# The opening's root mean squares: sums in all partitions, roots on full rows, no spread

## The chip, the cores and the metric

The kernel runs on one core of a Trainium2 chip. The metric is the device time of one execution in microseconds (us); of several runs the median is given. The engines are TensorE (PE in the profile, its weight loads PEld), VectorE (DVE), ScalarE (ACT), GpSimd (POOL) and SyncE (SP, whose queue issues the transfers). Each engine runs its own list of instructions in order; an instruction that waits holds up all that stand behind it on its engine.

## The reference

One encoder layer is applied to two groups of tokens, 2048 and 512, each with 16 learned meta tokens ahead. All of it is in f32.

```python
def rms_norm(x, g):
    x32 = x.astype(jnp.float32)
    y = x32 * lax.rsqrt(jnp.mean(x32 * x32, axis=-1, keepdims=True) + RMS_EPS)
    return (y * g.astype(jnp.float32)).astype(x.dtype)

def mixer_layer(h, norm_g, w_in, ...):
    u = rms_norm(h, norm_g)
    proj = u @ w_in
    qa, ka, va, za, qb, kb, vb, zb, ga, gb = jnp.split(proj, cuts, axis=-1)
    ... # neighbourhood attention on qa, ka, va; windowed attention on qb, kb, vb; gates; projections
```

The change is in how the first `rms_norm` gets its factor, the reciprocal root of each token's mean square over 1024 features.

## The kernel before

Features lie in partitions and tokens in columns, five windows of 512 tokens. A matrix is split into a high part in a short f32 format (fp32r) and the rest, and a product is three TensorE products: high by high, high by low, low by high (`mm3`, lines 146 to 148). The last window (number 4, with the meta tokens as 16 further columns) is projected alone; the first four go in pairs by Strassen's scheme.

The **opening** is the function `beside`: it projects window 4 for 22 tiles f of 128 output features (0 to 3 are qa, 4 to 7 qb, then ka, va, kb, vb), while VectorE and ScalarE make the Strassen operands of windows 0 and 1. One tile is 24 products in four steps of six, and the steps are counted in `q`. Two lists of step numbers in the call say when the generators `prep_last` (window 4's own preparation) and `prep_first` (that of windows 0 and 1) go on. The order on TensorE and in SP's queue is as written; the order on the other three engines is set when the program is built.

What the prediction touches:

- **Banks.** A tile's products add up in one of five PSUM banks (`ps_mm`, name `mm`). Window 4 is projected before it is normalised: the bank is emptied by `combine` (line 288), a VectorE product with `rs`, the row of factors, into `tq` or `tkv`. So no bank comes free before `rs` is there. Stores of the first tiles are held until step 14.
- **Weights.** A tile's weights land in `wraw`; ScalarE casts the high part and VectorE subtracts for the low part, in two halves (lines 207 and 208), into one of two buffers `wt`. Tile f+1's are made while f is projected, in the buffer of f-1.
- **The sums of squares.** ScalarE squares; VectorE adds up `rs` for window 4 (line 349) and `rsp` for window 0 (line 430), GpSimd `rsp` for window 1. The squares `sq` lie in the pool `ev`, four buffers that later also hold `evq`, the split queries on their way to memory.
- **The factors.** For window 4, `prep_last` at step 9 sums `rs` over the partitions by five f32 products with a column of ones, which put 128 tokens into partitions each; ScalarE copies the 128x5 sums; `rsqrt` (lines 153 to 163) takes the roots by three rounds on 128x5; `diagonal` (line 177) lays them on diagonals `rs_dg`; at step 14 five f32 products of ones with these (`spread`, line 185) put every token's factor into all partitions, and ScalarE copies it to `rs`. For windows 0 and 1, `prep_first` does the same at steps 20 and 27 with eight columns.
- **The operands.** From step 28 on VectorE scales windows 0 and 1 with these factors (line 384), adds and subtracts, and splits (388 and 389).

Of the kernel before, what the change touches and what calls it, by code (L numbers as in the profile page):

```python
# [17 lines left out]
P = 128  # L18
# [77 lines left out]
def encoder_block(ctx: ExitStack, tc: tile.TileContext, xT, x_end, w_in, w_pa, w_pb, w_o, norm_g, final_g,  # L96
# [25 lines left out]
    def f32(ap):  # L122
        return ap.bitcast(F32)
# [70 lines left out]

    wpool = ctx.enter_context(tc.tile_pool(name="wpool", bufs=2))
# [21 lines left out]
    class Weights:  # L217
# [12 lines left out]
        def split(self, i):  # L230
            if i < len(self.srcs):
                self.wt[i] = split_w(self.raw.pop(i))
# [91 lines left out]
    def prep_last(meta):  # L324
# [36 lines left out]
        nc.vector.tensor_add(rs[:, WTOK:], b[:, 0], b[:, 1])  # L361
        yield
        sq = st.tile([P, 32], F32, tag="sq", name="sq", bufs=1)[:, :5]
        nc.vector.memset(sq, 1.0)
        v = ps_t.tile([P, WTOK], F32, tag="vt", name="fin_v")
        for c in range(4):
            nc.tensor.matmul(v[:, c : c + 1], rs[:, c * P : (c + 1) * P], ones[:, 0:1], start=True, stop=True)
        nc.tensor.matmul(v[:N_META, 4:5], rs[:, WTOK:], ones[:, 0:1], start=True, stop=True)
        nc.scalar.copy(sq[:, :4], v[:, :4])
        nc.scalar.copy(sq[:N_META, 4:5], v[:N_META, 4:5])  # L370
        r = rsqrt(uxp, sq, P, 5)
        dgs = [ev.tile([P, WTOK], F32, tag="t", name="rs_dg", bufs=3) for _ in range(2)]
        diagonal(dgs[0], r[:, :4], P)
        diagonal(dgs[1], r[:N_META, 4:5], N_META)
        yield
        for dg, c0, m, nc_ in (dgs[0], 0, P, 4), (dgs[1], WTOK, N_META, 1):
            nc.scalar.copy(rs[:, c0 : c0 + nc_ * m], spread(ps_t, "vt", dg, m, nc_)[:, : nc_ * m])
# [26 lines left out]
    def prep_first(sp, wa, loaded):  # L404
# [27 lines left out]
        v = ps_t.tile([P, WTOK], F32, tag="vt", name="fin_v")  # L432
        for i in range(2):
            for c in range(4):
                nc.tensor.matmul(v[:, 4 * i + c : 4 * i + c + 1], rss[i][:, c * P : (c + 1) * P], ones[:, 0:1],
                                 start=True, stop=True)
        r = rsqrt(uxp, v[:, :8], P, 8)
        dgs = [ev.tile([P, WTOK], F32, tag="t", name="rs_dg", bufs=3) for _ in range(2)]
        for i in range(2):
            diagonal(dgs[i], r[:, 4 * i : 4 * i + 4], P)  # L440
        yield
        for i in range(2):
            nc.scalar.copy(rss[i], spread(ps_t, "vt", dgs[i], P, 4))
# [1358 lines left out]
```

## Time and profile before

| | before |
|---|---|
| median of 3 runs (lowest, highest) | 1874.19 us (1873.26, 1876.14) |
| the profiled execution | 1877.09 us, its span 1875.3 us |
| TensorE busy | 1852.4 us (99%) |
| VectorE, ScalarE, GpSimd busy | 1319.5, 1147.8, 778.4 us |
| first product of the opening | 7.22 us |
| first Strassen product | 123.52 us |

A row of the timeline gives the start in us from the span's beginning, the length in us, the engine, the line in the kernel, the operation, output and inputs, shapes and, behind an x, how many instructions were put together; in brackets the idle time ahead and what ended it. TensorE's instructions overlap: the distance of two starts is what one costs. A row of the waits gives who waited for whom, us in total, times, and the longest. Of a row by tile or line the three numbers are the shortest, median and longest duration in ns. A row by stretches gives the busy time of PE, PEld, DVE, ACT and POOL in this order, then the granted clock, the share of the transfer engines and GB/s.

### The profile page before, as it was taken

What the parts mean: (1) busy time and instruction counts of PE and PEld (TensorE: products, weight loads), DVE (VectorE), ACT (ScalarE), POOL (GpSimd) and SP (SyncE); (2) the same over time, 40 slices, a digit from 0 to 9 for tenths busy, and PEclk for the clock granted to TensorE, in tenths of its full rate; (3) what the DMA queues carried; (4) which work ended last, traced back from release to release, by engine and by line L of the source; (5) the groups of instructions that cost most, each with busy time, mean ns of one, the idle gap of its engine ahead of it and who ended that gap; (6) DMA issues with size and microseconds to landing.
All of it is one profiled execution on the core that took longest, in us unless ns stands there. A gap on an engine that the chain in (4) does not pass through costs nothing.

```text
span 1875.3 us, 29643 instructions
## 1 busy us (share of the span) xinstructions
PE 1852.4 (99%) x9755; PEld 1579.9 (84%) x9755; DVE 1319.5 (70%) x2914; ACT 1147.8 (61%) x2531; POOL 778.4 (42%) x599
## 2 busy tenths in 40 slices
PE   8999999999999999999999999999999999999998
PEld 6998888888888888888878888888888888888887
DVE  8886667556476565444457788878887877888874
ACT  6454444444365444444456797798789778878932
POOL 2015443323203232322324435657855874786420
PEclk9999999999999999999999999999999999999999
DMA  7565756655295677644258869968996997698483
GB/s 260 190 182 211 206 172 189 212 180 180 84 338 191 188 224 201 200 138 160 107 187 297 277 206 279 301 215 246 326 290 196 296 301 250 206 310 280 131 298 134
DMA packets 288145, 414.35 MB, mean 221 GB/s; under 512 B 117736, under 2 KB 162360, under 8 KB 286456
## 3 DMA queue, kind: packets, MB, share of 16 engines
q1 hardware_dynamic: 287704, 412.45, 68.6%
q8 instruction: 78, 1.28, 0.3%
q14 instruction: 75, 0.61, 0.1%
q10 hardware_dynamic: 288, 0.01, 0.0%
HBM read 303.46 MB, written 108.91 MB: 220 GB/s over the span
## 4 chain that ended last, share of the span: by engine, by line
PE 89%; DMA 5%; DVE 3%; ACT 1%; issue 1%; SPq 1%; ACTq 0%; DVEq 0%
PE pa L867 24%; PE pe L867 12%; PE pc L867 6%; PE mm L148 3%; PE mm L147 3%; PE mm L146 3%; PE pso L146 3%; PE pso L148 3%; PE pso L147 3%; PE tp L1283 3%; PE tp L1169 2%; PE psa L146 2%; PE psa L148 2%; PE psa L147 2%; PE psb L148 2%; PE psb L146 2%
## 5 line engine op out<-in xcount | busy, mean ns | idle before, releaser
L208 POOL TENSOR_TENSOR wt<-wraw,wt 128x512 fp32r<-128x512 f32 x164 | 212.3, 1314 | 249.1 <-ACT wt L207 233.0
L867 PE MATMUL pa<-u,wt 128*128 128x512 f32 x1008 | 242.8, 389 | 0.3 <-DVE wt L208 0.3
L867 PE MATMUL pa<-u,x 128*128 128x512 f32 x984 | 236.5, 389 | 0.0
L207 ACT CAST wt<-wraw 128x512 fp32r<-128x512 f32 x312 | 178.0, 619 | 76.8 <-DMA wraw<-in_w_in_dram 36.5
L867 PEld LDWEIGHTS pa<-u,wt 128*128 128x128 f32 x1008 | 189.0, 188 | 39.9 <-DVE wt L208 0.8
L867 PEld LDWEIGHTS pa<-u,x 128*128 128x128 f32 x984 | 184.7, 188 | 38.4
L836 POOL TENSOR_TENSOR s<-wraw,raw 128x512 f32<-128x512 f32 x40 | 58.3, 1458 | 277.2 <-DVE x L208 277.2
L146 PE MATMUL mm<-u,wt 128*128 128x512 f32 (+2 forms) x416 | 150.5, 362 | 7.2 <-ACT u L341 7.2
L147 PE MATMUL mm<-u,wt 128*128 128x512 f32 (+2 forms) x416 | 146.8, 353 | 1.0 <-DVE u L342 1.0
L148 PE MATMUL mm<-u,wt 128*128 128x512 f32 (+2 forms) x416 | 146.8, 353 | 0.3 <-DVE wt L208 0.2
L208 DVE TENSOR_TENSOR wt<-wraw,wt 128x512 fp32r<-128x512 f32 x148 | 104.8, 745 | 53.4 <-ACT wt L207 52.9
L867 PE MATMUL pe<-u,wt 128*128 128x512 f32 x504 | 121.3, 390 | 0.0
L867 PE MATMUL pc<-u,wt 128*128 128x512 f32 x504 | 121.1, 389 | 0.0
L867 PE MATMUL pe<-u,x 128*128 128x512 f32 x480 | 115.3, 389 | 0.0
L1172 ACT CAST ph<-tp 128x384 fp32r<-128x384 f32 (+6 forms) x160 | 81.8, 511 | 52.1 <-PE tp L1169 50.7
L841 POOL TENSOR_TENSOR s<-wraw,s 128x512 f32<-128x512 f32 x42 | 56.4, 1342 | 136.9 <-DVE wt L208 136.3
L867 PEld LDWEIGHTS pc<-u,wt 128*128 128x128 f32 x504 | 94.6, 188 | 19.6
L867 PEld LDWEIGHTS pe<-u,wt 128*128 128x128 f32 x504 | 94.5, 188 | 19.6
L146 PE MATMUL pso<-mh,wt 128*128 128x512 f32 x256 | 107.5, 420 | 0.0
L1068 DVE CUSTOM_DVE_ANT_0 s<-s,ba 128x384 f32<-128x384 f32 (+5 forms) x160 | 86.8, 543 | 29.1 <-PE s L1146 26.7
L1173 DVE TENSOR_TENSOR pl<-tp,ph 128x384 fp32r<-128x384 f32 (+6 forms) x160 | 94.9, 593 | 16.4 <-ACT ph L1172 13.6
L867 PEld LDWEIGHTS pe<-u,x 128*128 128x128 f32 x480 | 90.1, 188 | 18.7
(274 smaller groups left out, 5029.0 us busy)
## 6 DMA issues: line engine op xcount, KB each, us to landing
wraw<-in_w_in_dram SPq DMA_DIRECT2D x86, 512.0 KB
raw<-in_w_in_dram SPq DMA_DIRECT2D x40, 512.0 KB
q<-qa SPq DMA_DIRECT2D x40, 512.0 KB
wraw<-in_w_o_dram SPq DMA_DIRECT2D x32, 512.0 KB
kbt<-kb SPq DMA_DIRECT2D x32, 384.0 KB
qa<-evq SPq DMA_DIRECT2D x20, 512.0 KB
qb<-evq SPq DMA_DIRECT2D x20, 512.0 KB
ka<-evk SPq DMA_DIRECT2D x20, 512.0 KB
```

The lines of the kernel that those rows point to most:

```text
L146: nc.tensor.matmul(ps, wh, uh, start=first, stop=False)
L147: nc.tensor.matmul(ps, wh, ul, start=False, stop=False)
L148: nc.tensor.matmul(ps, wl, uh, start=False, stop=last)
L207: high[0] = nc.scalar.copy(h, r).ins
L208: low[0] = (eng or lo_eng[0]).tensor_sub(l, r, f32(h)).ins
L836: eng.tensor_sub(s3, a11, a21)
L841: eng.tensor_sub(s4, a12, s2)
L867: nc.tensor.matmul(ps, wt[:, a, s], u[:, b, kk, :], start=first and kk == 0 and i == 0, stop=kk == 3 and i == 2, skip_group_check=True)
L1068: nc.vector.tensor_tensor_reduce(s[:, :n], s[:, :n], bias, -1.0, 3.0e38, ALU.add, ALU.min, nm)
L1172: nc.scalar.copy(ph_[:kb, a], tb)
L1173: nc.vector.tensor_sub(pl_[:kb, a], tb, f32(ph_[:kb, a]))
L1283: nc.tensor.transpose(tp[:, c + h * P : c + (h + 1) * P], prs[:, k0[h] + j * P : k0[h] + (j + 1) * P], ident)
```

## The change

- Window 4: ScalarE and VectorE split `rs` into `rsh`. At step 10, not 9, two products of 512 columns of ones with the two parts (`by_ones`, lines 191 and 192) give the sums in all 128 partitions at once; the meta tokens' sums are an f32 product of 16 columns. At step 14, ScalarE makes the mean square `y` and -1/2 of it, `hv` (128x528); VectorE takes the roots on 128x528: one guess and three rounds of three operations. There is no diagonal, no spread and no copy.
- Windows 0 and 1: at step 20 the two sums are split into `rsq`; at step 22 four products with ones; then ScalarE makes the mean squares, VectorE the guesses, and two rounds of another iteration follow with five steps on ScalarE and five on GpSimd for each window. The spread at step 27 goes.
- In `dense_fin`, later in the kernel, only names change.

```diff
+    def guess(r, ve):
+        nc.vector.tensor_scalar(r.bitcast(I32), ve.bitcast(I32), -0.5, float(0x5F3759DF), ALU.mult, ALU.add)
...
         nc.vector.tensor_add(rs[:, WTOK:], b[:, 0], b[:, 1])
-        yield
-        sq = st.tile([P, 32], F32, tag="sq", name="sq", bufs=1)[:, :5]
-        nc.vector.memset(sq, 1.0)
-        v = ps_t.tile([P, WTOK], F32, tag="vt", name="fin_v")
-        for c in range(4):
-            nc.tensor.matmul(v[:, c : c + 1], rs[:, c * P : (c + 1) * P], ones[:, 0:1], start=True, stop=True)
-        nc.tensor.matmul(v[:N_META, 4:5], rs[:, WTOK:], ones[:, 0:1], start=True, stop=True)
-        nc.scalar.copy(sq[:, :4], v[:, :4])
-        nc.scalar.copy(sq[:N_META, 4:5], v[:N_META, 4:5])
-        r = rsqrt(uxp, sq, P, 5)
-        dgs = [ev.tile([P, WTOK], F32, tag="t", name="rs_dg", bufs=3) for _ in range(2)]
-        diagonal(dgs[0], r[:, :4], P)
-        diagonal(dgs[1], r[:N_META, 4:5], N_META)
-        yield
-        for dg, c0, m, nc_ in (dgs[0], 0, P, 4), (dgs[1], WTOK, N_META, 1):
-            nc.scalar.copy(rs[:, c0 : c0 + nc_ * m], spread(ps_t, "vt", dg, m, nc_)[:, : nc_ * m])
+        e = ev.tile([P, 2, WTOK], F32R, tag="ev", name="rsh")
+        split(e[:, 0, :], e[:, 1, :], rs[:, :WTOK])
+        yield
+        v = by_ones(ps_t, "vt", e[:, 0, :], e[:, 1, :], "fin_v")
+        vm = ps_t.tile([P, WTOK], F32, tag="vt", name="fin_m")[:, :N_META]
+        nc.tensor.matmul(vm, ones, rs[:, WTOK:], start=True, stop=True)
+        y, hv = (ev.tile([P, 2, WTOK], F32, tag="ev", name=n).rearrange("p i t -> p (i t)")[:, :UW]
+                 for n in ("rsy", "rshv"))
+        for dst, k in (y, 1.0), (hv, -0.5):
+            nc.scalar.activation(dst[:, :WTOK], v, AF.Copy, bias=k * EPS, scale=k / D_MODEL)
+            nc.scalar.activation(dst[:, WTOK:], vm, AF.Copy, bias=k * EPS, scale=k / D_MODEL)
+        guess(rs, y)
+        for _ in range(3):
+            nc.vector.tensor_mul(y, rs, hv)
+            nc.vector.tensor_mul(y, y, rs)
+            nc.vector.scalar_tensor_tensor(rs, y, 1.5, rs, ALU.add, ALU.mult)
+        yield
         yield
...
-        v = ps_t.tile([P, WTOK], F32, tag="vt", name="fin_v")
+        parts = []
         for i in range(2):
-            for c in range(4):
-                nc.tensor.matmul(v[:, 4 * i + c : 4 * i + c + 1], rss[i][:, c * P : (c + 1) * P], ones[:, 0:1],
-                                 start=True, stop=True)
-        r = rsqrt(uxp, v[:, :8], P, 8)
-        dgs = [ev.tile([P, WTOK], F32, tag="t", name="rs_dg", bufs=3) for _ in range(2)]
+            e = ev.tile([P, 2, WTOK], F32R, tag="ev", name="rsq")
+            split(e[:, 0, :], e[:, 1, :], rss[i])
+            parts.append((e[:, 0, :], e[:, 1, :]))
+        yield
         for i in range(2):
-            diagonal(dgs[i], r[:, 4 * i : 4 * i + 4], P)
-        yield
-        for i in range(2):
-            nc.scalar.copy(rss[i], spread(ps_t, "vt", dgs[i], P, 4))
+            v = by_ones(ps_t, "vt", *parts[i], "fin_v")
+            nc.scalar.activation(tts[:, i], v, AF.Copy, bias=EPS, scale=1.0 / D_MODEL)
+            guess(rss[i], tts[:, i])
+        temps = [ev.tile([P, 2, WTOK], F32, tag="ev", name="rt") for _ in range(2)]
+        both = [(rss[i], tts[:, i], temps[i][:, 0], temps[i][:, 1]) for i in range(2)]
+        mul, act = nc.gpsimd.tensor_mul, nc.scalar.activation
+        for step in (lambda r, ve, y, t: act(y, r, AF.Square), lambda r, ve, y, t: mul(y, y, ve),
+                     lambda r, ve, y, t: act(t, y, AF.Copy, scale=0.375, bias=-1.25), lambda r, ve, y, t: mul(t, t, y),
+                     lambda r, ve, y, t: act(t, t, AF.Copy, bias=1.875), lambda r, ve, y, t: mul(r, r, t),
+                     lambda r, ve, y, t: act(y, r, AF.Square), lambda r, ve, y, t: mul(y, y, ve),
+                     lambda r, ve, y, t: act(y, y, AF.Copy, scale=-0.5, bias=1.5), lambda r, ve, y, t: mul(r, r, y)):
+            for each in both:
+                step(*each)
         yield
...
-        begun = beside(firsts, raws, wts, (own, (9, 14)), 0, steps, [2, 20, 27, *(28 + 27 * i // 10 for i in range(16))],
+        begun = beside(firsts, raws, wts, (own, (10, 14)), 0, steps, [2, 20, 22, *(28 + 27 * i // 10 for i in range(16))],
                        zeros)
```

The build sets the order on three engines anew. Beyond the opening the order is the same as before. Three places:

**TensorE, window 4's sums.** Before, in the third tile, behind its first step:

```order
L148 MATMUL mm<-u_292,wt 128x512
L367 MATMUL fin_v<-ones,rs_294 128x1 x4
L368 MATMUL fin_v<-ones,rs_294 16x1
L146 MATMUL mm<-u_292,wt 128x512
L147 MATMUL mm<-u_293,wt 128x512
```

After, one step later:

```order
L148 MATMUL mm<-u_292,wt 128x512
L191 MATMUL fin_v<-rsh,ones 128x512
L192 MATMUL fin_v<-rsh,ones 128x512
L370 MATMUL fin_m<-rs_294,ones 128x16
L146 MATMUL mm<-u_292,wt 128x512
L147 MATMUL mm<-u_293,wt 128x512
```

Nothing stands at step 14 any more, where the spread was. The four products with rsq stand together two steps into the sixth tile (f=5).

**VectorE, around the first rows that empty banks.** Names with numbers tell tiles apart. Before, wt_595 and wt_666 are the weights of f=5 and f=6, mm_371 is f=0's bank, mm_436 f=1's:

```order
L430 TENSOR_TENSOR rsp0_348<-rsp0_348,sq_406 128x512 x2
L288 TENSOR_TENSOR tq_559<-mm_371,rs4_294 128x512
L288 TENSOR_TENSOR tq_565<-mm_436,rs4_294 128x512
L430 TENSOR_TENSOR rsp0_348<-rsp0_348,sq_410 128x512
L208 TENSOR_TENSOR wt_595<-wraw_466,wt_595 128x512 x2
L254 TENSOR_TENSOR evq_561<-tq_559,evq_561 128x8x4x16
```

After, wt_579 and wt_626 are those of f=5 and f=6, and mm_374 is f=0's bank. The first round of window 4's roots (lines 378 to 380) ends here and the second begins:

```order
L434 TENSOR_TENSOR rsp0_351<-rsp0_351,sq_413 128x512
L211 TENSOR_TENSOR wt_579<-wraw_469,wt_579 128x512
L379 TENSOR_TENSOR rsy_492<-rsy_492,rs4_294 128x528
L380 SCALAR_TENSOR_TENSOR rs4_294<-rsy_492,rs4_294 128x528
L211 TENSOR_TENSOR wt_626<-wraw_525,wt_626 128x512 x2
L378 TENSOR_TENSOR rsy_492<-rs4_294,rshv_493 128x528
```

Five more rows of the roots follow (379, 380, and 378 to 380 again), and then:

```order
L291 TENSOR_TENSOR tq_543<-mm_374,rs4_294 128x512
L291 TENSOR_TENSOR tq_549<-mm_439,rs4_294 128x512
L257 TENSOR_TENSOR evq_545<-tq_543,evq_545 128x8x4x16
L257 TENSOR_TENSOR evq_551<-tq_549,evq_551 128x8x4x16
L291 TENSOR_TENSOR tq_555<-mm_474,rs4_294 128x512
L291 TENSOR_TENSOR tq_573<-mm_530,rs4_294 128x512
L257 TENSOR_TENSOR evq_557<-tq_555,evq_557 128x8x4x16
L257 TENSOR_TENSOR evq_575<-tq_573,evq_575 128x8x4x16
L291 TENSOR_TENSOR tq_620<-mm_589,rs4_294 128x512
L257 TENSOR_TENSOR rsq_614<-rsp0_351,rsq_614 128x512
L257 TENSOR_TENSOR rsq_617<-rsp1_352,rsq_617 128x512
```

The first row that empties a bank (tq of f=0) has moved from ahead of f=5's weights to behind f=6's, and the pieces rsq stand behind the first five tq.

**ScalarE, ahead of the roots.** Before, the copies of the spread rows stand behind the last squares (sq) of window 0:

```order
L425 ACTIVATE sq_406<-x2_352 128x1024
L425 ACTIVATE sq_410<-x2_352 128x1024
L377 COPY rs4_294<-rs_rb_550 128x512
L377 COPY rs4_294<-rs_rb_556 128x16
L207 CAST wt_595<-wraw_466 128x512 x2
L253 CAST evq_561<-tq_559 128x8x4x16
```

After, the four rows that make y and hv stand there, and the casts of f=5's and f=6's weights follow at once; rsh stands ahead of all squares, ten rows earlier:

```order
L429 ACTIVATE sq_413<-x2_355 128x1024
L374 ACTIVATE rsy_492<-fin_v_487 128x512
L375 ACTIVATE rsy_492<-fin_m_490 128x16
L374 ACTIVATE rshv_493<-fin_v_487 128x512
L375 ACTIVATE rshv_493<-fin_m_490 128x16
L210 CAST wt_579<-wraw_469 128x512 x2
L210 CAST wt_626<-wraw_525 128x512 x2
L256 CAST evq_545<-tq_543 128x8x4x16
```

The buffer that `rsy` takes in `ev` is that of the fourth square, which GpSimd reads last; `rsq` takes those of the first two `evq`.

More of the change, by code (lines that the diff above doesn't have):

```diff
@@ L1436, in dense_fin @@
     def dense_fin(w):
-        ssq, pool = acc["s", w], nc.gpsimd
+        ssq = acc["s", w]
         def spare(i, dtype, name):
@@ L1445, in dense_fin @@
         nc.scalar.copy(sh, ssq)
-        pool.tensor_sub(sl, ssq, f32(sh))
+        nc.gpsimd.tensor_sub(sl, ssq, f32(sh))
         yield
@@ L1452, in dense_fin @@
         nc.scalar.activation(ve, v, AF.Copy, bias=EPS, scale=1.0 / D_MODEL)
-        nc.vector.tensor_scalar(r.bitcast(I32), ve.bitcast(I32), -0.5, float(0x5F3759DF), ALU.mult, ALU.add)
-        mul, ts = pool.tensor_mul, pool.tensor_scalar
+        guess(r, ve)
+        mul, ts = nc.gpsimd.tensor_mul, nc.gpsimd.tensor_scalar
         for steps in ((lambda: mul(y, r, ve), lambda: mul(y, y, r)),
```

## The prediction

> **What bounds the kernel now.** I read the engine totals first, then TensorE's own waits up to 160 us, then the timelines of the first 60 us, where every edit of the change lies.
>
> ```profile
> PE 1852.4 (99%) x9755; PEld 1579.9 (84%) x9755; DVE 1319.5 (70%) x2914; ACT 1147.8 (61%) x2531; POOL 778.4 (42%) x599
> PE mm L146 <- ACT u L341: 7.2, 1, 7.2
> PE rs_rb L185 <- DVE rs_dg L177: 1.0, 1, 1.0
> PE pa L867 <- DVE wt L208: 0.3, 1, 0.3
> ```
>
> TensorE is busy for 1852.4 of 1875.3 us. In the first 160 us it waits for its first operands (7.2 us), 1.0 us for the spread of the last window's roots, and hardly otherwise. So a microsecond taken from its queue in the opening is a microsecond of the kernel, as long as the other engines still deliver in time; and a wait put into that queue costs its full length, since no idle time later takes it back.
>
> **What goes from TensorE.** Rows of its timeline (start, length, instruction); each group of three is the last product ahead of an edit, the edit, and the second product behind it.
>
> ```profile
> 22.53 0.39 PE L148 MATMUL mm<-u,wt 128*128 128x512 f32 x1
> 22.76 0.95 PE L367 MATMUL fin_v<-ones,rs 128*128 128x1 f32 x8
> 24.10 0.40 PE L147 MATMUL mm<-u,wt 128*128 128x512 f32 x1
> 30.47 0.39 PE L148 MATMUL mm<-u,wt 128*128 128x512 f32 x1
> 31.87 1.48 PE L185 MATMUL rs_rb<-rs_dg,ones 128*128 128x128 f32 x10 [1.01 <-DVE rs_dg L177]
> 33.61 0.40 PE L147 MATMUL mm<-u,wt 128*128 128x512 f32 x1
> 41.34 0.39 PE L148 MATMUL mm<-u,wt 128*128 128x512 f32 x1
> 41.57 1.84 PE L435 MATMUL fin_v<-ones,rsp 128*128 128x1 f32 x16
> 43.59 0.40 PE L147 MATMUL mm<-u,wt 128*128 128x512 f32 x1
> 52.48 0.39 PE L147 MATMUL mm<-u,wt 128*128 128x512 f32 x1
> 52.71 0.40 PE L148 MATMUL mm<-u,wt 128*128 128x512 f32 x1
> 52.94 1.95 PE L185 MATMUL rs_rb<-rs_dg,ones 128*128 128x128 f32 x16
> 54.96 0.39 PE L147 MATMUL mm<-u,wt 128*128 128x512 f32 x1
> ```
>
> Products of 512 columns follow each other every 0.23 us (52.48 to 52.71; 0.2274 over many). Without the edit, the third row of a group would start 0.455 us behind the first. So the four edits cost 1.57 - 0.455 = 1.12, 3.14 - 0.455 = 2.69 (its wait of 1.01 included), 2.25 - 0.455 = 1.80 and 1.80 again: **7.4 us go**.
>
> **What comes to TensorE.** The same two products with ones stand later in this kernel, for windows 2 and 3:
>
> ```profile
> L191 PE MATMUL fin_v<-xq,ones x2: 392/393/394, 290.0 to 290.4; 128*128 128x512 f32 x2
> L192 PE MATMUL fin_v<-xq,ones x2: 392/396/399, 290.2 to 290.7; 128*128 128x512 f32 x2
> 23.63 0.20 PE L368 MATMUL fin_v<-ones,rs 128*16 128x1 f32 x2
> ```
>
> They start 0.23 us apart, so six of them take 1.4 us. The product for the meta tokens is in plain f32, 16 columns; the nearest row, two records in 0.20 us, with some 0.1 us on going from one kind to the other, gives 0.3 us. **1.7 us come** (1.5 to 1.9). If that were all, the change would gain 5.7 us.
>
> **The first new wait: f=5's bank.** Products of the tiles f = 0, 1, ... go into five banks, so f=5 needs that of f=0, which the row tq (the product times rs) empties. I follow both sides.
>
> TensorE, unhindered: up to 22.76 as before; then eleven steps of six products (10 to 20) take 15.0 us, and the sums with ones 0.9, so the last product of f=4 starts at 38.4 and f=5 wants to start at 38.65.
>
> Vector side: the order on VectorE after the change puts tq for f=0 behind all three rounds of the roots, and the last two rounds behind the weight rows of f=6 (wt_626). These weights lie in the buffer of f=4's, so ScalarE's cast for them begins when f=4's last product is over. The rows of before show that very step:
>
> ```profile
> 41.81 1.14 ACT L207 CAST wt<-wraw 128x512 fp32r<-128x512 f32 x2 [3.06 <-PE mm L148]
> 42.77 1.29 DVE L208 TENSOR_TENSOR wt<-wraw,wt 128x512 fp32r<-128x512 f32 x2
> 16.43 1.42 DVE L349 TENSOR_TENSOR rs<-rs,xt 128x512 f32<-128x512 f32 x2
> 36.76 1.28 DVE L288 TENSOR_TENSOR tq<-mm,rs 128x512 f32<-128x512 f32 x2
> 43.27 0.49 PE L146 MATMUL mm<-u,wt 128*128 128x512 f32 x1
> ```
>
> The cast starts 0.47 us behind the start of f=4's last product (41.34) and its halves end 0.62 and 1.14 us later; VectorE takes 0.60 us a half. Now: 38.4 + 0.47 + 1.14 = 40.0 for the second cast, 40.7 for the second half on VectorE. Behind it stand six root operations on 528 columns, each waiting for the one ahead: dependent additions of 512 columns stand 0.71 us apart (1.42 for two), so 0.73 each, 4.4 in all: 45.1. tq adds 0.7: f=0's bank is free at 45.8. **That is 7.2 us after f=5 wanted it.** In before the same tq ran at 36.76, and f=5 began at 43.27: it had some six microseconds to spare. Now the chain hangs on f=4's own end, so nothing earlier can shorten it.
>
> It can be longer, when VectorE reaches wt_626 late. What stands ahead begins with the sums:
>
> ```profile
> 18.96 3.48 DVE L349 TENSOR_TENSOR rs<-rs,xt 128x512 f32<-128x512 f32 x2
> 20.28 3.30 POOL L430 TENSOR_TENSOR rsp<-rsp,sq 128x512 f32<-128x512 f32 x2
> 25.83 5.43 POOL L430 TENSOR_TENSOR rsp<-rsp,sq 128x512 f32<-128x512 f32 x4 [2.25 <-ACT sq L425]
> L1453 DVE TENSOR_SCALAR rbs<-ve x3: 408/410/410, 1283.8 to 1618.7; 128x512 int32<-128x512 int32 x3
> ```
>
> VectorE and GpSimd hinder each other: two additions took 3.48 us beside GpSimd's, 1.42 alone. ScalarE now makes rsh ahead of the squares, so GpSimd cannot begin before it: the sum ends at 18.96 + 1.42 = 20.4, rsh at 21.0, the first square at 22.1, and seven GpSimd additions at 1.36 (5.43 / 4) to 1.65 (3.30 / 2) end at 31.6 to 33.7. ScalarE's rsy takes the buffer of the fourth square and waits for the last of them; with 0.8 us of its own, the first guess on VectorE (0.41) starts at 32.4 to 34.5, and seven more rows of 0.6 to 0.73 end at 37.5 to 40. The first half of wt_626 is ready at 39.5: the two chains meet. A VectorE held up further by GpSimd adds 0 to 2 us. I take **8.0 us** (6.5 to 9).
>
> **The second new wait: the pieces of the other two sums.** TensorE restarts at R = 46.6. Two steps later (R + 2.7) come the four products with ones for windows 0 and 1. Their pieces rsq take the buffers of the first two evq, so they wait until these are stored.
>
> ```profile
> 39.76 0.69 DVE L254 TENSOR_TENSOR evq<-tq,evq 128x512 fp32r<-128x512 f32 x1
> 48.19 3.34 DMA va<-zr
> ```
>
> From tq on: evq's cast 0.6 and subtraction 0.7 end at R + 1.4; the store takes up to 3.3 us (the chain's row for a smaller store; 2.5 as the lower bound, a little under it); rsq's cast and subtraction 1.3: R + 5.2 to R + 6.0. The second pair is some 1.2 us behind, so the last product ends at R + 6.7 to R + 7.5, not at R + 3.6: **3.5 us** (2 to 4.5).
>
> The first ten products of the kernel, after 7.2 us of idling, ran at 0.43 us instead of 0.23 (their start rows are 11.16 and 11.59 below). After a stall of 8 us I expect such a slow stretch again, 10 x 0.2 = 2 us; but it falls into the 3.5 us in which TensorE would wait for rsq anyway. I add 0 (up to 2).
>
> ```profile
> 11.16 0.63 PE L148 MATMUL mm<-u,wt 128*128 128x512 f32 x1
> 11.59 0.63 PE L146 MATMUL mm<-u,wt 128*128 128x512 f32 x1
> ```
>
> [...]
>
> **The third: VectorE behind.** Roots of windows 0 and 1 start when the sums are there, at R + 7.4 = 54: 1.7 us on ScalarE and VectorE, then ten GpSimd products.
>
> ```profile
> L1413 POOL TENSOR_TENSOR ssq<-ssq,xres 128x512 f32<-128x512 f32 x28 | 36.2, 1292 | 0.0
> 56.09 1.41 DVE L384 SCALAR_TENSOR_TENSOR x<-x,ng,rsp 128x512 f32<-128x512 f32 x2
> 60.00:80.00 20.00, 19.66 (x151) 18.73 (x150) 18.40 (x35) 11.10 (x21) 0.00 (x0) 1.00 0.55 181
> 80.00:100.00 20.00, 20.00 (x166) 19.98 (x166) 20.00 (x45) 9.84 (x20) 0.00 (x0) 1.00 0.62 203
> 100.00:120.00 20.00, 20.00 (x167) 19.94 (x166) 18.53 (x37) 9.99 (x21) 0.00 (x0) 1.00 0.66 146
> ```
>
> At 1.29 to 1.65 us each they end at 69 to 72. The scaling of the operands, at 56.09 before, starts some 14 us later, while TensorE is then 6 to 8 us later than before. VectorE (the third busy column, 18.40, 20.00 and 18.53 of 20) has only 3.1 us free from 60 to 120, so 3 to 5 us of its lag must show: weight halves that stand among the scaling rows come late to TensorE. I take **3 us** (0 to 5).
>
> **The sum.** -7.4 + 1.7 + 8.0 + 3.5 + 3.0 = +8.8 us. Low ends: -7.4 + 1.5 + 6.5 + 2 + 0 = +2.6; high ends: -7.4 + 1.9 + 9 + 4.5 + 5 = +13. The profiled execution took 1877.09 us, 1.8 of them outside its span; the median shown is 2.9 below it, 1874.19. On the profile's own time the sum gives 1885.9, on the median **1883.0 us**, by its own terms 1876.8 to 1887.
>
> **Rivals.**
> - *The products are all that counts* (faster). If f=0's bank is free by 38.65, TensorE pays no new wait: 1874.2 - 5.7 = 1868.5. For it: the bank had six microseconds to spare. Against: two rounds of roots and two weight halves between f=4's end and tq. It needs VectorE to get past them in 0.2 us. 0.12.
> - *Half of it* (no change). Only f=5 waits, at the low end, and the rest hides: -5.7 + 6.5 = +0.8, 1875. For it: TensorE's lead gives ScalarE and the stores time. Against: rsq stands behind tq, not behind the sums. 0.09.
> - *VectorE becomes the bound.* Two additions beside GpSimd cost 2.06 us more; ten GpSimd products can so add some 7 to 10 us to VectorE's work with 3.1 us free: the third term is 10 instead of 3, 1890. It decides if VectorE lags until the first Strassen products near 130 us. 0.12.
> - *The slow clock is paid in full.* If rsq is ready early, the slow products cost their 2 us: 1885. 0.10. [...]
>
> **How the numbers follow.** The forecast has the rest, 0.57. Slower by over 0.2% (3.7 us, about what a measurement tells from no change): forecast and the last two rivals, 0.79. Within: 0.09. Faster: 0.12. The range leaves out the faster case and a few per cent of the worst: 1875.5 to 1888.5.
>
> **What would show it.** In TensorE's waits: a stall of 7 to 9 us at L146 for VectorE's tq near 39 us; 2 to 4.5 us at L191 and L192 for rsq; a few of about 1 us at L148 for weight halves from 70 to 110 us; no wait at a spread. The first Strassen product (L867, 123.52 before) would start near 132. I am wrong if f=5 starts below 41 us, or if that product starts before 123.

## The result and the profile after

The change makes the kernel slower. In the first comparison its median is 1888.45 us of 6 runs (1882.97 to 1892.66) beside 1875.99 of the kernel before on the same chip; the ratio is 1.0055, 95% interval 1.0035 to 1.0075, which is +10.3 us (6.6 to 14.1). In a second comparison the ratio is 1.0069 (1.0050 to 1.0088), +13 us. The medians themselves lie further apart than the first ratio says, 12.5 us in the first comparison and 12.4 in the second (1889.99 and 1877.59). The forecast was 1883.0, in a range of 1875.5 to 1888.5: the median lies at the upper edge of that range.

The waits of TensorE in the first 160 us of the kernel after, longest first (total, how often, the longest one):

```profile
PE mm L146 <- DVE tq L291: 8.3, 1, 8.3
PE mm L146 <- ACT u L344: 7.3, 1, 7.3
PE mm L148 <- DVE wt L211: 1.8, 3, 0.7
PE fin_v L192 <- DVE rsq L257: 0.9, 1, 0.9
PE pa L879 <- DVE wt L211: 0.7, 1, 0.7
PE fin_v L191 <- ACT rsq L256: 0.3, 1, 0.3
```

The second row is the wait for the first operands, as before. All others are new in size; the wait at a spread is gone. TensorE's timeline around them, from f=4's last product to the end of the products with ones for windows 0 and 1:

```profile
38.24 0.39 PE L148 MATMUL mm<-u,wt 128*128 128x512 f32 x1
46.90 0.77 PE L146 MATMUL mm<-u,wt 128*128 128x512 f32 x1 [8.27 <-DVE tq L291]
47.46 0.63 PE L147 MATMUL mm<-u,wt 128*128 128x512 f32 x1
49.99 0.40 PE L147 MATMUL mm<-u,wt 128*128 128x512 f32 x1
51.57 0.50 PE L191 MATMUL fin_v<-rsq,ones 128*128 128x512 f32 x1 [0.25 <-ACT rsq L256]
52.99 0.50 PE L192 MATMUL fin_v<-rsq,ones 128*128 128x512 f32 x1 [0.92 <-DVE rsq L257]
53.94 0.40 PE L146 MATMUL mm<-u,wt 128*128 128x512 f32 x1
```

TensorE's last product of f=4 starts at 38.24, and 0.39 us later it stands still for 8.27 us. One row of ScalarE and VectorE's timeline say on what:

```profile
32.05 1.77 DVE L434 TENSOR_TENSOR rsp<-rsp,sq 128x512 f32<-128x512 f32 x1
38.67 1.14 ACT L210 CAST wt<-wraw 128x512 fp32r<-128x512 f32 x2 [3.05 <-PE mm L148]
40.41 1.28 DVE L211 TENSOR_TENSOR wt<-wraw,wt 128x512 fp32r<-128x512 f32 x2
41.61 0.70 DVE L378 TENSOR_TENSOR rsy<-rs,rshv 128x528 f32<-128x528 f32 x1
45.32 0.71 DVE L380 SCALAR_TENSOR_TENSOR rs<-rsy,rs 128x528 f32<-128x528 f32 x1
46.06 1.29 DVE L291 TENSOR_TENSOR tq<-mm,rs 128x512 f32<-128x512 f32 x2
52.26 1.28 DVE L257 TENSOR_TENSOR rsq<-rsp,rsq 128x512 fp32r<-128x512 f32 x2
70.18 2.44 DVE L388 SCALAR_TENSOR_TENSOR x<-x,ng,rsp 128x512 f32<-128x512 f32 x2 [0.59 <-POOL rsp L453]
```

f=6's weight halves, then the last two rounds of the roots (six operations, 0.74 us apart), then tq, then, behind the stores of the queries, rsq: the order of the prediction, with its durations row by row. One thing differs. ScalarE had cast the first of f=6's halves some 0.6 us into its row, near 39.3, but VectorE came to it only at 40.41: it had been busy almost without a pause (16.95 of the 17.23 us from 28.83 to 46.06), and three of its rows beside GpSimd's additions, which run until 33.27, had taken 1.6 to 1.8 us (the first row above is one) in place of 0.7. In windows (busy time and records of TensorE, its loads, VectorE, ScalarE and GpSimd, then granted clock, share of the transfer engines, GB/s), the kernel before and the kernel after:

```profile
40.00:60.00 20.00, 20.00 (x106) 17.10 (x105) 15.39 (x35) 5.64 (x10) 0.00 (x0) 1.00 0.64 219
```

```profile
40.00:60.00 20.00, 11.93 (x43) 9.05 (x44) 16.29 (x27) 8.64 (x16) 3.10 (x3) 0.83 0.54 189
```

TensorE is busy 8.1 us less in this stretch. Two landmarks cut the rest: the first Strassen product (pa), and the first product of the attention (s), behind the Strassen stage. In the kernel before and after:

```profile
123.52 2.92 PE L867 MATMUL pa<-u,wt 128*128 128x512 f32 x12
978.73 0.34 PE L1145 MATMUL s<-kd,q 128*128 128x216 f32 x1 [0.21 <-PE mm L148]
```

```profile
131.12 2.92 PE L879 MATMUL pa<-u,wt 128*128 128x512 f32 x12
988.62 0.52 PE L1157 MATMUL s<-kd,q 128*128 128x216 f32 x1 [0.22 <-PE mm L148]
```

The opening ends 131.12 - 123.52 = 7.6 us later, the Strassen stage takes 857.5 instead of 855.2 us, 2.3 more, and from there to the end it is 896.7 against 896.6. That is the whole of the 10.0 us between the two spans (1885.3 and 1875.3).

### The profile page after: what moved, and what is told of

It is laid out like the page before. It is cut to its first block, busy times and chain, and to the rows that moved or that the text cites. A ratio compares the mean times of both kernels' runs of the same rounds, so it can differ in the third digit from the quotient of the medians.

```text
span 1885.3 us, 29571 instructions
## 1 busy us (share of the span) xinstructions
PE 1852.8 (98%) x9711; PEld 1578.9 (84%) x9711; DVE 1323.8 (70%) x2898; ACT 1155.8 (61%) x2544; POOL 793.9 (42%) x609
## 3 DMA queue, kind: packets, MB, share of 16 engines
q8 instruction: 78, 1.28, 0.3%
## 4 chain that ended last, share of the span: by engine, by line
PE 89%; DVE 4%; DMA 3%; ACT 1%; issue 1%; POOL 1%; SPq 0%; DVEq 0%; ACTq 0%; POOLq 0%
PE pa L879 23%; PE pe L879 12%; PE pc L879 6%; PE pso L146 3%; PE pso L148 3%; PE pso L147 3%; PE tp L1181 3%; PE tp L1295 2%; PE mm L148 2%; PE mm L147 2%; PE mm L146 2%; PE psb L148 2%; PE psb L146 2%; PE psb L147 2%; PE psa L146 2%; PE psa L148 2%
## 5 line engine op out<-in xcount | busy, mean ns | idle before, releaser
L146 PE MATMUL mm<-u,wt 128*128 128x512 f32 (+2 forms) x416 | 151.8, 365 | 15.6 <-DVE tq L291 8.3
L147 PE MATMUL mm<-u,wt 128*128 128x512 f32 (+2 forms) x416 | 148.4, 357 | 2.4 <-DVE u L345 2.4
L148 PE MATMUL mm<-u,wt 128*128 128x512 f32 (+2 forms) x416 | 148.4, 357 | 1.8 <-DVE wt L211 1.8
```

The costliest lines, as they stand in the source:

```text
L146: nc.tensor.matmul(ps, wh, uh, start=first, stop=False)
L147: nc.tensor.matmul(ps, wh, ul, start=False, stop=False)
L148: nc.tensor.matmul(ps, wl, uh, start=False, stop=last)
```

## The experiments

What is to be told apart: is it the **chain on VectorE** (weight halves, roots, tq, then evq and rsq) that TensorE waits for, as predicted, and does it cost in full; is it VectorE's or GpSimd's **total work**; what does the **slow clock** behind the wait cost; and where do the 2 us behind the opening come from?

In the table pa is the start of the first Strassen product, s - pa the length of the Strassen stage, both from one profile; the ratio is to the kernel before on the same chip. The kernels with a single run have no ratio; only their timelines are read.

| kernel | pa, us | s - pa, us | ratio (95%) |
|---|---|---|---|
| before, two profiles | 123.52, 122.55 | 855.2, 855.5 | |
| the whole change, two profiles | 131.12, 131.34 | 857.5, 857.5 | 1.0055, 1.0069 |
| window 4 alone | 128.95 | 856.2 | 1.0028 (1.0012 to 1.0045) |
| windows 0 and 1 alone | 124.91 | 857.4 | 1.0018 (1.0004 to 1.0033) |
| six banks | 132.43 | 857.7 | one run, 1890.39 us |
| two rounds | 129.03 | 857.6 | 1.0052 (1.0035 to 1.0069) |
| kept busy | 133.11 | 857.5 | one run, 1898.29 us |
| square root | 127.58 | 857.3 | 1.0043 (1.0030 to 1.0056) |
| square root, window 4 alone | 125.91 | 857.8 | 1.0019 (1.0007 to 1.0031) |
| window 4 alone, kept busy | 129.77 | 856.4 | one run, 1890.37 us |
| square root, late columns, two profiles | 121.23, 121.27 | 858.3, 856.8 | 1.0027 (1.0016 to 1.0038), 1.0014 (1.0003 to 1.0026) |

### Window 4 alone

```
 # windows 0 and 1 as before: sums by columns, rsqrt on 128x8, diagonals, spread at step 27
-begun = beside(firsts, raws, wts, (own, (10, 14)), 0, steps, [2, 20, 22, ...], zeros)
+begun = beside(firsts, raws, wts, (own, (10, 14)), 0, steps, [2, 20, 27, ...], zeros)
```

> The change for the last window (4) alone; windows 0 and 1 keep their sums by columns and their spread from the kernel before. My theory (TensorE waits at f=5 for tq of f=0, which stands on VectorE behind f=6's weight halves and the last two rounds of the roots): the wait at f=5 is still there and ends at the same time, 46 to 47.5 us from the start, where f=5 began at 43.27 before; so this part alone costs 3 to 4 us, and some 1 to 1.5 us of slow products behind the stall, which no wait for rsq hides now. The first Strassen product starts at 127.0 to 129.0 (123.52 before, 131.12 with the whole change); ratio to the kernel before 1.002 to 1.003. Rival A (the wait at f=5 belongs to the new roots of windows 0 and 1, by GpSimd's load on VectorE): f=5 starts before 42 us and the first Strassen product near 120.5; ratio 0.9984. Rival B (the slow clock is paid nowhere): f=5 as in my theory, first Strassen product at 126.5 to 127.

TensorE's timeline of this kernel:

```profile
47.03 0.76 PE L146 MATMUL mm<-u,wt 128*128 128x512 f32 x1 [6.39 <-DVE tq L291]
52.70 0.40 PE L147 MATMUL mm<-u,wt 128*128 128x512 f32 x1
59.30 1.95 PE L185 MATMUL rs_rb<-rs_dg,ones 128*128 128x128 f32 x16
```

f=5 starts at 47.03, as with the whole change; that TensorE waits 6.4 instead of 8.3 us for it is only because the columns of windows 0 and 1 now stand in front. So the wait is window 4's own, and rival A is out. What was under-sized is the slow clock: 13 products from 47.03 to 52.70 take 5.67 us where they should take 2.96 (13 x 0.2274). It costs 2.7 us, not 1 to 1.5, and nothing hides it here; rival B is out too. pa at 128.95 and the ratio are in the expected ranges.

### Windows 0 and 1 alone

```
 # window 4 as before: sums by columns at step 9, rsqrt on 128x5, diagonals, spread at step 14
-begun = beside(firsts, raws, wts, (own, (10, 14)), 0, steps, [2, 20, 22, ...], zeros)
+begun = beside(firsts, raws, wts, (own, (9, 14)), 0, steps, [2, 20, 22, ...], zeros)
```

> The change for windows 0 and 1 alone; the last window keeps its sums by columns, its roots in columns and its spread. My theory: no wait at f=5 (tq of f=0 runs near 37 us as before); TensorE saves 3.6 us of columns and spread and gets 0.9 us of products; it waits 1 to 3 us for the pieces rsq at the products with ones and, since VectorE has twenty-odd us of work from GpSimd's ten products and the late scaling, 1 to 4 us in pieces of under 1 us for weight halves. The first Strassen product starts at 123 to 127; ratio 1.000 to 1.002. Rival A (all the loss is the wait at f=5): no waits of note, the first Strassen product near 121, ratio 0.9986. Rival B (VectorE behind is the main cost): more than 6 us of waits for weight halves, the first Strassen product at 128 or later, ratio 1.0025 or more.

No wait at f=5; 1.3 us at L192 for rsq, 1.6 us in five pieces and 0.7 at the first Strassen product for weight halves. pa is 1.9 us later than the mean of the two profiles of before. That is within my range and rules out both rivals: this part does not pay, but it is not the main loss. The two parts add up: 5.9 us (window 4 alone) and 1.9 are 7.8, against 8.2 for the whole change, all by pa and the means of two profiles where there are two.

### Six banks

```
-    ps_mm = ph.enter_context(tc.tile_pool(name="ps_mm", bufs=5, space=PSUM))
-    ps_t = ph.enter_context(tc.tile_pool(name="ps_t", bufs=3, space=PSUM))
+    ps_mm = ph.enter_context(tc.tile_pool(name="ps_mm", bufs=6, space=PSUM))
+    ps_t = ph.enter_context(tc.tile_pool(name="ps_t", bufs=2, space=PSUM))
```

> The whole change, with six banks for the products of the tiles and two for the sums instead of five and three, so that f=5 doesn't need the bank of f=0. My theory (both waits hang on the same chain on VectorE: roots, then tq, evq, rsq): f=5 starts at 38 to 39 us without a wait, and TensorE waits instead 9 to 12 us at the products with ones for rsq; these end at 53 to 55 as with the whole change, and the first Strassen product starts at 130 to 133 (131.12 with the whole change). Rival (the bank itself is what costs): the 8 us are gone, the waits for rsq stay at 1 to 4 us, the first Strassen product starts at 122 to 126.

Its waits:

```profile
PE fin_v L191 <- ACT rsq L256: 10.2, 1, 10.2
PE fin_v L192 <- DVE rsq L257: 0.6, 1, 0.6
```

The 8.3 us at f=5 are gone, and 10.2 us stand at the next place that hangs on the same chain. pa is at 132.43. The bank is where the wait shows, not what it costs.

### Two rounds

```
-        for _ in range(3):
+        for _ in range(2):
             nc.vector.tensor_mul(y, rs, hv)
             nc.vector.tensor_mul(y, y, rs)
             nc.vector.scalar_tensor_tensor(rs, y, 1.5, rs, ALU.add, ALU.mult)
```

> The whole change, with two rounds of the last window's roots instead of three: the third round, which only improves the digits, is left out. Three operations of 0.73 us, one behind the other, go from the chain on VectorE ahead of tq. My theory: the wait at f=5 is 2.2 us shorter (6.1 instead of 8.3) and all later waits start from there, so the first Strassen product starts at 128.5 to 129.5 (131.12 with the whole change); ratio 1.004. Rival (VectorE's load with GpSimd's share, not this chain, sets the lag, or the weight halves of f=6 arrive too late for it to matter): the first Strassen product stays within 0.7 us of 131.1, and waits for weight halves take the place; ratio 1.0055.

```profile
44.82 0.77 PE L146 MATMUL mm<-u,wt 128*128 128x512 f32 x1 [6.24 <-DVE tq L291]
```

f=5 starts 46.90 - 44.82 = 2.08 us sooner and pa 2.1 us sooner (129.03): three operations of VectorE are worth their full length to TensorE. The ratio's interval holds both theories; the verdict rests on the timeline.

### Kept busy

```
+        idle = ps_t.tile([P, WTOK], F32, tag="vt", name="idle")
+        for n in range(34):
+            nc.tensor.matmul(idle, ones_r, us[NWIN - 1][0][:, n % KT, :WTOK], start=True, stop=True)
+        yield
         for i in range(2):
             v = by_ones(ps_t, "vt", *parts[i], "fin_v")
...
-begun = beside(firsts, raws, wts, (own, (10, 14)), 0, steps, [2, 20, 22, ...], zeros)
+begun = beside(firsts, raws, wts, (own, (10, 14)), 0, steps, [2, 20, 20, 22, ...], zeros)
```

> The whole change, and behind f=4's products 34 more products with ones into a bank of their own, whose result nothing uses: 34 x 0.2274 = 7.7 us of TensorE work inside the 8.3 us in which it waits for tq. They show what the slow clock behind that wait costs. My theory (the slow products are hidden, since TensorE must wait for rsq anyway): the granted clock from 40 to 60 us goes from 0.83 to near 1.00, f=5 starts at 46.5 to 47.5 as with the whole change, its products are 0.23 us apart at once, the wait for rsq at the products with ones grows by 1.0 to 1.5 us, and the first Strassen product stays at 130.5 to 132. Rival (the slow clock is paid in full): the products with ones and the first Strassen product come 1 us or more earlier, at 130.1 or before.

```profile
38.46 8.10 PE L444 MATMUL idle<-u,ones 128*128 128x512 f32 x34
46.89 0.47 PE L146 MATMUL mm<-u,wt 128*128 128x512 f32 x1 [0.34 <-DVE tq L291]
47.20 0.40 PE L147 MATMUL mm<-u,wt 128*128 128x512 f32 x1
51.58 0.49 PE L191 MATMUL fin_v<-rsq,ones 128*128 128x512 f32 x1 [1.69 <-ACT rsq L256]
52.98 0.79 PE L192 MATMUL fin_v<-rsq,ones 128*128 128x512 f32 x1 [0.91 <-DVE rsq L257]
54.43 0.63 PE L146 MATMUL mm<-u,wt 128*128 128x512 f32 x1
```

f=5 starts at the same time, and its products stand 0.23 us apart from the second on (47.20 to 47.43) instead of 0.43. The first product with ones still starts at 51.58 (51.57 without), the last ends 0.5 us later. So in the whole change the slow products behind the stall cost nothing: TensorE spends the time waiting for rsq otherwise. The second profile of the change says the same: there the slow products last 5.1 us (47.14 to 52.27) and not 3.1, and from f=5's start to the end of the products with ones it is 7.06 us, as in the first (7.04). I had expected a granted clock near 1.00; it was 0.91, since a new slow stretch begins behind the two waits of 1.69 and 0.91 us (products 0.43 us apart from 53.58 to 56.14). pa is 2.0 us later than without, outside my range; the order of the rows on VectorE behind this place differs from that of the change too (three scaling rows stand earlier), so I don't read more from it.

### Window 4 alone, kept busy

The same, in the kernel with window 4's part alone, 27 products:

```
+        idle = ps_t.tile([P, WTOK], F32, tag="vt", name="idle")
+        for n in range(27):
+            nc.tensor.matmul(idle, ones_r, us[NWIN - 1][0][:, n % KT, :WTOK], start=True, stop=True)
+        yield
...
-begun = beside(firsts, raws, wts, (own, (10, 14)), 0, steps, [2, 20, 27, ...], zeros)
+begun = beside(firsts, raws, wts, (own, (10, 14)), 0, steps, [2, 20, 20, 27, ...], zeros)
```

> The change for the last window alone, with 27 more products with ones (27 x 0.2274 = 6.1 us, result unused) in the 6.4 us in which TensorE waits at f=5. In the run without them the first twelve products behind the wait stood 0.43 us apart instead of 0.23, and from f=5's start (47.03) to the spread of windows 0 and 1 (59.30) went 12.3 us, against 9.7 in the kernel before; no wait for rsq hides that. My theory (the slow clock behind the wait costs TensorE those 2.6 us): with the products f=5 starts at 46.5 to 47.5 as without, and the spread comes 9.6 to 10.0 us later, near 57; the first Strassen product then at 126 to 127.5 (128.95 without them), or up to 128.8 if weight halves, which VectorE brings no sooner, take it back. Rival (the stretch is slow for another reason, such as late loads of weights): the spread stays 12 us behind f=5.

```profile
46.80 0.47 PE L146 MATMUL mm<-u,wt 128*128 128x512 f32 x1
56.43 1.95 PE L185 MATMUL rs_rb<-rs_dg,ones 128*128 128x128 f32 x16
```

From f=5 to the spread it is 9.63 us instead of 59.30 - 47.03 = 12.27. So the slow clock does cost 2.6 us where no other wait covers it. But pa came at 129.77, not sooner, and outside both ranges that I had given: TensorE lost it again between 60 and 70 us, to weights (3.0 us of waits). Three rows of this kernel, from SP's queue and from ScalarE, show how, and behind them two of SP's queue in the kernel before and two in the kernel after:

```profile
62.08 0.32 SPq L142 DMA_DIRECT2D qb<-evq  x1
62.44 0.43 SPq L142 DMA_DIRECT2D wraw<-in_w_in_dram  x1
66.62 1.14 ACT L210 CAST wt<-wraw 128x512 fp32r<-128x512 f32 x2 [2.65 <-DMA wraw<-in_w_in_dram]
```

```profile
40.48 5.20 SPq L142 DMA_DIRECT2D qa<-evq  x4
45.73 0.65 SPq L142 DMA_DIRECT2D wraw<-in_w_in_dram  x1
```

```profile
48.21 3.88 SPq L142 DMA_DIRECT2D qa<-evq  x4
52.14 0.65 SPq L142 DMA_DIRECT2D wraw<-in_w_in_dram  x1
```

The loads of raw weights (wraw) stand in SP's queue behind the stores of the queries (qa, qb), and these wait for the products with the roots. So a late tq also makes the weights late (52.14 instead of 45.73), ScalarE waits for them, and a TensorE that is faster in between only waits too: the cast at 66.62 stands at 66.75 in the kernel without the 27 products. I had not thought of that queue.

### Square root

```
-        y, hv = (ev.tile([P, 2, WTOK], F32, tag="ev", name=n).rearrange("p i t -> p (i t)")[:, :UW]
-                 for n in ("rsy", "rshv"))
...
+        y = ev.tile([P, 2, WTOK], F32, tag="ev", name="rsy").rearrange("p i t -> p (i t)")[:, :UW]
+        nc.scalar.activation(y[:, :WTOK], v, AF.Copy, bias=EPS, scale=1.0 / D_MODEL)
+        nc.scalar.activation(y[:, WTOK:], vm, AF.Copy, bias=EPS, scale=1.0 / D_MODEL)
+        nc.scalar.activation(y, y, AF.Sqrt)
+        nc.vector.reciprocal(rs, y)
```

> The whole change, but the last window's roots by one square root on ScalarE and one reciprocal on VectorE in place of the guess and the nine operations of three rounds. VectorE loses 0.43 + 9 x 0.71 = 6.8 us in the chain ahead of tq and gets one reciprocal of 528 columns, whose price no row shows (0.7 us like the others at least); ScalarE gets the root, 0.6 us, and two loads of tables at 1.28 us, by the profile's row for such loads. My theory (that chain is what TensorE waits for): f=5's wait falls from 8.3 to between 0 and 4 us; rsq and the weight halves still cost 1 to 4; the first Strassen product starts at 123 to 127.5 (131.12 with the whole change), ratio 1.000 to 1.0025. Rival (VectorE's load by GpSimd's products and adds sets the end): the first Strassen product at 129 or later, ratio 1.004 or more.

> The change for the last window alone, with its roots by ScalarE's square root and VectorE's reciprocal; windows 0 and 1 as in the kernel before. If the chain ahead of tq is the cause, this keeps the saving of window 4's columns and spread (1.12 + 2.69 us, less 0.73 us for the new products) and pays only what is left of the wait at f=5, 0 to 3 us, and 0 to 1 us for the columns of windows 0 and 1, which now come early: the first Strassen product starts at 120.5 to 124.5 (123.52 before); ratio 0.998 to 1.0015. Rival (window 4's new work on VectorE and ScalarE costs as much in any form): the first Strassen product at 126 or later, ratio 1.002 or more.

The rows of the first of the two kernels, ScalarE and VectorE:

```profile
34.86 1.28 ACT L374 ACT_TABLE_LOAD   x1
36.15 0.65 ACT L374 ACTIVATE rsy<-rsy 128x528 f32<-128x528 f32 x1
38.11 3.45 DVE L375 RECIPROCAL rs<-rsy 128x528 f32<-128x528 f32 x1
```

A reciprocal of 528 columns takes 3.45 us, five times a product of two rows, so half of the saving on VectorE went. f=5 waited 5.0 us (0 to 4 expected), and pa came at 127.58, a hair outside my range, 3.5 us sooner than with the change. With window 4 alone the wait was 3.3 us, pa 125.91 (124.5 at most expected) and the ratio 1.0019 (1.0015 at most): both miss my ranges and lie just under the rival's marks of 126 and 1.002. The chain is confirmed by its direction, not by my sizes. The ratio of the first, 1.0043, is in the rival's range; of its +8 us (5.6 to 10.5) the opening explains only 4.5 and the Strassen stage 2.0.

### Square root, late columns

Against the kernel with the square root for window 4 alone:

```
-        y = ev.tile([P, 2, WTOK], F32, tag="ev", name="rsy").rearrange("p i t -> p (i t)")[:, :UW]
+        y = ev.tile([P, UW], F32, tag="t", name="rsy", bufs=3)
...
-begun = beside(firsts, raws, wts, (own, (10, 14)), 0, steps, [2, 20, 27, ...], zeros)
+begun = beside(firsts, raws, wts, (own, (10, 14)), 0, steps, [2, 23, 27, ...], zeros)
```

> The last window's part alone, with ScalarE's square root and VectorE's reciprocal; rsy in a tile of its own instead of the buffer of a square, so that ScalarE need not wait for GpSimd's last addition; and the columns of windows 0 and 1 three steps later, in the middle of f=5. If the chain ahead of tq of f=0 is what eats the gain, this takes it off TensorE's path: rsy starts some 1.4 us sooner, the reciprocal stands ahead of the last additions for rsp and of the weight halves of f=6, and tq of f=0 runs before TensorE asks for f=5. My theory: no wait for tq, no slow stretch, at most 2 us of waits for a weight half that now stands behind the reciprocal; TensorE keeps 3.81 - 0.73 = 3.1 us less what these waits take: the first Strassen product at 119.5 to 122.5 (122.55 and 123.52 in two profiles of the kernel before), ratio 0.998 to 0.9995, the first version faster than the kernel before. Rival (VectorE's total work, not the order of this chain, is what TensorE pays for): the wait moves to the weight halves and is 3 us or more; the first Strassen product at 123.5 or later, ratio 1.000 or more.

```profile
35.17 0.50 PE L148 MATMUL mm<-u,wt 128*128 128x512 f32 x1 [1.62 <-DVE wt L211]
```

In the opening everything is as expected: no wait for tq, one of 1.62 us for a weight half behind the reciprocal, pa at 121.23, 1.8 us before the mean of the kernel before. So the products with ones do save TensorE some 3 us (1.8 and the 1.6 of that wait), once the chain is off its path. Yet the kernel is slower than before, by 0.27%: pa is where my theory put it, and the ratio where the rival did. Which is the last question.

### Behind the opening: two second profiles and one of the kernel before

> The kernel before, unchanged, for a second profile of it. In all profiles of changed kernels so far, between 960 and 1100 us TensorE's granted clock falls to 0.91 to 0.98 in two stretches of 20 us, behind waits of some 1.5 us, and 2 to 5 us are lost there; in the first profile of the kernel before it stays at 1.00. If that is chance, the second profile of the kernel before may show it too: a stretch at 0.91 to 0.98 between 980 and 1100 and a span of 1877 to 1882. If it comes from the change, the second profile shows 1.00 throughout and a span within 2 us of 1875.3.

> The whole change, unchanged, for a second profile. Open is what lies behind the opening. There, from the first Strassen product to the first product of the attention, the two profiles of the kernel before took 855.2 and 855.5 us, the first one of the whole change 857.5; from there to the end 896.6, 900.4 and 896.7. If the 2 us of the Strassen stage belong to the change, they are there again (857 to 858); if they are chance, the second profile may show 855 to 856. The opening should repeat: the first Strassen product at 130.5 to 132; ratio 1.004 to 1.007.

> The version with square root, reciprocal and late columns, unchanged, for a second profile and more times. Its opening was 1.3 to 2.3 us shorter than that of the kernel before (first Strassen product at 121.23), yet its time 1.0027 of it; its Strassen stage took 858.3 us against 855.2 and 855.5. If what follows an earlier opening really gives the gain back, the Strassen stage is 857 or more again and the ratio 1.001 or more; if that was chance, it is 855 to 856.5 and the ratio 0.998 to 1.001. The first Strassen product at 120.7 to 122 in both cases.

The kernel before, second profile, and the kernel after, second profile, from 1060 to 1080 us (TensorE's busy time and records, granted clock, share of the transfer engines, GB/s):

```profile
1060.00:1080.00 20.00, 18.34 (x94) 0.91 0.80 253
```

```profile
1060.00:1080.00 20.00, 18.69 (x108) 1.00 0.96 305
```

This slow stretch in the attention is chance: the kernel before has it in its second profile, the change not in its second. Another one, from 980 to 1000 us, may belong to the change: the granted clock is 0.91 there in both of its profiles, behind the two waits shown below, and 1.00 in both of the kernel before. The second span of the kernel before is 1878.5, 3.2 above the first, all of it behind s (900.4 against 896.6).

The Strassen stage is not chance: 855.2 and 855.5 us in the kernel before, 857.5 and 857.5 in the change, and 856.2 to 858.3 in all the others. In the change it can be placed. From the first Strassen product to the second block of products into pc (at 141.13 us in the kernel before) it takes 17.6 and 17.7 us in the kernel before, 18.1 and 17.8 in the change; from there to the last tile of products (mm) it takes 830.8 us in all four profiles; and that tile, up to s, takes 6.8 and 7.0 us before, 8.6 and 8.9 in the change. So nearly all of it lies in this last tile. TensorE meets two waits there, not one (0.69 and 0.84 us in the profiles of the kernel before), for the operands of the last window, which is prepared once more. In the kernel after:

```profile
984.52 0.50 PE L147 MATMUL mm<-u,wt 128*128 128x512 f32 x1 [0.69 <-DVE u L345]
986.98 0.50 PE L147 MATMUL mm<-u,wt 128*128 128x512 f32 x1 [1.49 <-DVE u L345]
```

The change's second profile has the same two (0.71 and 1.49 us). In it SP issues the loads of xt for these operands at 972.05 us, in the kernel before at 962.26. That is 9.8 us later, when TensorE's last tile starts 8.0 later. The kernel before and the kernel after, second profile:

```profile
961.30 0.87 SPq L142 DMA_DIRECT2D wraw<-in_w_in_dram  x2
962.26 1.94 SPq L142 DMA_DIRECT2D xt<-in_xT_dram  x4
```

```profile
969.30 2.65 SPq L142 DMA_DIRECT2D wraw<-in_w_in_dram  x2
972.05 1.93 SPq L142 DMA_DIRECT2D xt<-in_xT_dram  x4
```

The further 1.8 us lie in one place: two loads of raw weights just ahead hold SP for 2.65 us (2.81 in the first profile) instead of 0.87. No row shows why the second of them takes so long to be issued.

The version with late columns had the shorter opening again (121.27), a Strassen stage of 856.8, just under the 857 that I had set as the mark, and a ratio of 1.0014: slower both times, in keeping with a gain that is given back. Its stage from pa to s took 1.3 to 3 us longer than in the kernel before. Of that, 1.0 to 1.2 us are gone by that second block into pc (18.8 and 18.6 us): TensorE waits there for weight halves twice, 0.95 us in all, and in the kernel before once, 0.34. In its first profile TensorE also waits 0.34 us for ScalarE, ahead of 310.77 us. What took the rest is open. No version tried beats the kernel before.

## Why the prediction was right

**Direction, place and price of the first wait: right.** The first new wait was put at f=5's bank, near 39 us, at 8.0 us (6.5 to 9); it starts at 38.6 and is 8.27. The chain named for it ran in the named order: f=6's weight halves, six root operations, tq. That TensorE pays for what stands ahead of tq on VectorE is shown by taking three operations out (2.1 us gained). It is not the bank (with one more, the wait moves on), and not the new roots of windows 0 and 1 on GpSimd (window 4 alone has the same wait, and in the change they start only at 55.95 us). But of the two ways to be late that the prediction let meet, VectorE's own backlog ended last: it came to f=6's halves at 40.41, some 1.1 us behind ScalarE's cast. So "nothing earlier can shorten it" does not hold for that last microsecond, to which GpSimd's additions beside VectorE contribute, and the 0.8 us that the sum put on top of 7.2 had the right reason.

**What goes and comes: right.** The products with ones and the meta product of window 4 cost 0.7 us (forecast: two at 0.23 and one at 0.3), and the version that takes the chain off the path shows the saving.

**The second new wait: right, in sum and in why.** From f=5's restart to the end of the products with ones it is 53.94 - 46.90 = 7.04 us; 12 products and four with ones would take 3.64. So 3.4 us, forecast 3.5 (2 to 4.5). The slow clock was booked at 0 (up to 2) because the wait for rsq covers it. The kept-busy run and the second profile show that cover, and window 4 alone what the slow clock costs without it: 2.6 us. The rival "The slow clock is paid in full" was thus near on the price (2 us) and wrong on the cover.

**The third, VectorE behind: right in kind, a little too large.** Scaling starts at 70.18, 14 us later than before, and GpSimd's products end at 71.4, both as forecast. But TensorE waits 1.8 us for weight halves, three times 0.6 on average, and 0.7 at the first Strassen product, 2.5 in all; 0.5 of that kind stood in the kernel before (0.2 and 0.3), so 2.0 are new, in place of the 3.0 of the sum. VectorE is busy 39.9 of the 40 us from 80 to 120, but most halves were still in time. The rival "VectorE becomes the bound" put this term at 10 us.

**What the sum missed: the Strassen stage.** The sum ended at the first Strassen product and took all behind it to be only shifted. There the change costs another 2.1 us (857.5 against the mean of 855.2 and 855.5), twice. So the +8.8 of the forecast is 8.2 in the opening (mean of two profiles each) and 2.1 behind it, 10.3 in all. That this is just the first ratio's +10.3 is partly luck: its interval is 6.6 to 14.1, and the second ratio says 13. Behind s the two profiles of the kernel before differ by 3.9 us from each other, so nothing smaller can be read there. The median lies 5.4 us above the forecast: 1.5 by this sum and 1.8 by the kernel before, whose median over more runs was 1875.99 and not 1874.19; the remaining 2.1 is less than the spread of the runs. That the median still fell into the range, at its very edge, owes something to luck too: the range was not made for a loss behind the opening.

**Not settled:** why SP needs 1.8 us more for the two loads ahead of the last tile of the Strassen stage; what, beyond the weight halves at its start, takes back the shorter opening of the last version; and what lies behind s.

## What to carry to other kernels

Work that is taken from the bound engine is gained only if the engines behind it still deliver in the order in which it asks; here VectorE's ten full-row operations ahead of the first tq brought a wait of 8.3 us, more than the 7.4 us of products and spread that the whole change took away. When a wait disappears after a change to its buffer, look at once for the next place that hangs on the same chain (here 8.3 us became 10.2), and follow the queue of transfers too: a store that waits there holds up the loads behind it (here weights issued at 45.73 us before came at 52.14). Measure a kernel like this to its end: an opening that was 1.8 us shorter gave no shorter time.

## What the runs showed of the hardware

- **The slow clock had no fixed price.** Behind a stall of 8.3 us TensorE's products stood 0.43 us apart, in place of 0.23, for 3.1 us in the first profile of the change (46.90 to 49.99) and for 5.1 us in the second of the same kernel (47.14 to 52.27); behind the 6.4 us of window 4 alone it was 5.7 us (47.03 to 52.70). It also came behind two waits of 1.69 and 0.91 us with one product between them (kept busy, to 56.14), and did not come behind one of 1.62 us (late columns, products 0.23 us apart from 35.51 on). What brings such a stretch on and what sets its length, no run shows.
- **A reciprocal on VectorE took 3.45 us** for 128x528 (square root, and again with window 4 alone), against 0.71 us for a product of two such rows. GpSimd was not beside it: ScalarE's rsy, which waits for GpSimd's additions, starts at 33.14, the reciprocal at 38.11 (square root).
- **Loading a table for ScalarE took 1.28 us.** In the square-root version ScalarE's cast ahead ends at 34.84 us, the load runs from 34.86, and the root starts at 36.15.
